# Loading x in contiguous pieces and reordering the front of a state-space mixer kernel

## The chip, the core and the metric

The kernel runs on one core of a Trainium2 chip. The core has five instruction queues that run side by side: TensorE (PE, matrix products), VectorE (DVE), ScalarE (ACT), GpSimd (POOL) and SyncE (SP, which here only issues DMA transfers). Each works through its own instructions in the order in which they are written; they meet through semaphores. The metric is the device time of one execution, in microseconds (us), as the median of several runs. All data is float32.

## The reference

One layer of a diffusion backbone: an S5 state-space mixer over 256 context and 1024 latent tokens in both directions, then a gated output, then a SwiGLU feed-forward part, each behind an RMS norm whose shift, scale and gate come from the conditioning vector. Cut to what matters here:

```python
def rms_norm(x, g):
    return x * rsqrt(mean(x * x, axis=-1) + 1e-6) * g

m_l = split(silu(c)     @ ada_w + ada_b, 6)      # latent tokens
m_c = split(silu(c_ctx) @ ada_w + ada_b, 6)      # context tokens
h_l = rms_norm(x,   norm_mix) * (1 + m_l[1]) + m_l[0]
h_c = rms_norm(ctx, norm_mix) * (1 + m_c[1]) + m_c[0]

def s5_direction(u_ctx, u_lat, ...):             # 64 groups of 16 channels, 64 states each
    lam_bar = exp(lam * exp(log_step))
    b_bar   = (lam_bar - 1) / lam * (b_re + 1j * b_im)
    def run(u, h0):                              # h[t] = lam_bar * h[t-1] + b_bar @ u[t]
        ...                                      # y[t] = Re(c_mat @ h[t])
    y_c, h_c = run(u_ctx, 0)
    y_l, _   = run(u_lat, h_c)                   # the latent scan starts from the context's state

y = (forward + backward) + d * h
g = gelu(y); y = g * sigmoid(g @ w_glu + b_glu)
x = x + m_l[2] * y
h = rms_norm(x, norm_ffn) * (1 + m_l[4]) + m_l[3]
x = x + m_l[5] * ((silu(h @ w1) * (h @ w3)) @ w2)   # 1024 -> 2816 -> 1024
out = rms_norm(x, norm_final)
```

## The kernel before, in words

**Layout.** The token sequence is cut into chunks of 8 sub-steps (T = 8): 128 chunks of x and 32 of the context. A partition row stands for one of 8 sub-steps times 16 channels. The array `U` (in the tile `ru`, 40 KB in each partition) holds for each of the 64 groups 160 columns: 32 of the context, then 128 of x. Eight groups make a *unit* of 5 KB; unit b of `U` is what the later products read.

**Order.** Nothing is scheduled by a planner: the order in which the code is written is the order on each engine, and the tables `PMUL`, `UACT`, `UCTX`, `RSL` and so on say in which turn a step is issued. Tiles that share memory are kept apart by semaphore waits that follow from the order.

**The front** (L150 to L575) does the following.

- SP issues, in this order, lambda (L152), `xT` in four transfers of 1 MB (L156) that land directly in the x columns of `U`, so in pieces of 512 bytes, `ctxT` of 1 MB into `rxa` (L158), the input matrices `bxy`, and `ada_w` in eight transfers of 512 KB (`ada1_load(0)`, L172), and then eight more.
- Row sums of squares, ten tiles (eight of x, two of the context): ACT squares (L204), POOL adds the two halves of each tile, PE multiplies by a block of ones and adds up over the tiles (L206, one product of 512 columns a tile, into `psx` and `psc`). DVE folds the four column groups (L323, L324), one ACT square root for both (L325), DVE reciprocals `rsp` (L535) and `rcp` (L544).
- Modulation rows: `ada1(0, k)`, two PE products for each k (L199), k = 0..7, as the loads arrive.
- Eigenvalues: a long chain of small DVE operations gives lambda-bar; `cmul` then makes by complex products its powers `PW` and the products `CP` = c times lambda-bar^k, in seven calls of four instructions each.
- `lb_dup` (PE L331, ACT L332) spreads `CP` over the partitions as `LB`. `bl_make(hb)` multiplies `LB` (copied by `lb_psum` at L426 or L428) with the input matrices, two 128x1024 products on DVE or, for the half units in `PMUL`, on POOL; `bl_sum` adds them; `bl_tr` (PE L443, ACT L446) transposes the sum into the weights of `sums`.
- `mix_rows`, `mix_turn`, `mix_scale`, `mix_sel`, `mix_cols` (L456, L460, L77, L475/L476, L481) turn the modulation rows into columns of shift and scale.
- `rs_lat(b)` multiplies unit b's x columns by 1/rms (DVE, 128x1024, in place). The context columns are moved from `rxa` into `U` by the same kind of product, units 0 and 1 at one time (L545) and the other six later (L720). `u_act` (ACT L497), `u_lat` (DVE) and `u_ctx` (POOL) then apply scale and shift.

**The sixteen half units.** A loop over hb = 0..15 (a unit has a forward and a backward half) runs, each turn: `sums(hb)` (PE L584 in two parts, evicted by ACT at L590 or L592/L593), `bl_tr(hb + 2)`, `rs_lat` of a later unit where `RSL = {0: 2, 1: 3, 3: 4, 5: 5, 6: 6, 8: 7}` says so, `u_act` and `u_ctx` of a unit by `UACT` and `UCTX`, `pair` (the first step of the scan, on DVE or POOL), `bl_sum(hb + 5)` (a DMA that adds, issued by POOL, L433) and `bl_make(hb + 6)`. At hb = 6 and 8 `pw_full` (PE L386, ACT L388) writes the spread powers `PWF` into the first 4 KB of `rxa`, where `ctxT` was.

**The rest.** After the loop the scan over chunks runs on DVE, then come the output products, the gated part and the feed-forward part, in which PE works.

Of the kernel before, what the change touches and what calls it, by code (L numbers as in the profile page):

```python
# [13 lines left out]
AF = mybir.ActivationFunctionType  # L14
OP = mybir.AluOpType
AX = mybir.AxisListType

P = 128
D = 1024
# [4 lines left out]
T = 8  # L24
G = 64
# [17 lines left out]
def s5_ffn_kernel(tc, a, out):  # L43
# [3 lines left out]
    with ctx:  # L47
# [107 lines left out]
        for h in range(4):  # L155
            SY.dma_start(X[:, 16 * h:16 * h + 16], a["xT"][:, 16 * h:16 * h + 16])  # L156
        ctxT = view(RXa, 0, [G, 32])
# [35 lines left out]
        psx, psc = pw([4, P]), pw([16, 32])  # L193
# [6 lines left out]

        for i in range(10):
            src = X[:, 8 * i:8 * i + 8] if i < 8 else ctxT[:, 32 * i - 256:32 * i - 224]
            jk, po = junk[i % 6], psx if i < 8 else psc
            S.activation(jk.rearrange("p a b -> p (a b)").rearrange("p (g c) -> p g c", c=src.shape[2]), src, AF.Square)  # L204
# [71 lines left out]
        CP = view(RA, 5.5, [T, 2, G])  # L276
# [5 lines left out]
        qi = PW[:, 0, 1]  # L282
# [4 lines left out]
        ts(PW[:, 0, 0], pr, 1.0, ADD)  # L287
# [8 lines left out]
        def cmul(o, x, tmps=(LTa, view(RXc, 0, [256]))):  # L296
# [15 lines left out]

        V.tensor_copy(yb, PW[:, 0])
# [10 lines left out]
        V.tensor_reduce(rsc, psc.rearrange("p g c -> p c g"), AX.X, ADD)  # L324
        S.activation(rsb, rsb, AF.Sqrt, bias=epsc[:, 0:1], scale=1.0 / D)  # L325
# [10 lines left out]
        cmul(PW[:, 7:8], PW[:, 3:4])  # L336
        ada1(0, *range(3, 8))
# [152 lines left out]
        def rs_lat(b):  # L490
            if b < 8:
                gs = slice(8 * b, 8 * b + 8)
                tt(X[:, gs], X[:, gs], bc(rsp, 1, 8), MUL)
# [41 lines left out]
        V.reciprocal(rsp, rsx)  # L535
        rs_lat(0)
        bl_make(1)
# [1222 lines left out]
```

## Time and profile before

| | |
|---|---|
| three runs | 1019.77, 1023.63, 1024.74 us; median 1023.63 us |
| profiled execution | span 1023.7 us from first to last instruction; this is the only time that the page gives for it |
| busy share of the span | PE 94%, PEld 76%, DVE 77%, POOL 75%, ACT 43% |
| mean granted TensorE clock | 0.985 of full speed |
| moved by DMA | 98.95 MB, mean 97 GB/s |

A row of the timeline reads: start, length, engine, line, operation, what is written and what is read, how many instructions are joined in the row, and in brackets the idle time of the engine just before the row and what ended it. "L77" and "L80" are the lines of helpers (two- and three-operand vector operations), so those rows are told apart by their tiles: `ru` is `U`, `rxa` holds `ctxT` and later `PWF`, `c` are the four work regions, `lta`, `ltb`, `lbt` are PSUM tiles with constants. A row of a table of stages gives, for a stretch of time, the busy time of each engine with its number of instructions, then the granted TensorE clock, the mean busy share of the 16 DMA engines and the GB/s that they moved. "PEld" is the loading of weights into TensorE, beside PE.

### The profile page before, as it was taken

What the parts mean: (1) busy time and instruction counts of PE and PEld (TensorE: products, weight loads), DVE (VectorE), ACT (ScalarE), POOL (GpSimd) and SP (SyncE); (2) the same over time, 40 slices, a digit from 0 to 9 for tenths busy, and PEclk for the clock granted to TensorE, in tenths of its full rate; (3) what the DMA queues carried; (4) which work ended last, traced back from release to release, by engine and by line L of the source; (5) the groups of instructions that cost most, each with busy time, mean ns of one, the idle gap of its engine ahead of it and who ended that gap; (6) DMA issues with size and microseconds to landing.
All of it is one profiled execution on the core that took longest, in us unless ns stands there. A gap on an engine that the chain in (4) does not pass through costs nothing. (4 is left out here: it accounts for less than half of the span.)

```text
span 1023.7 us, 18545 instructions
## 1 busy us (share of the span) xinstructions
PE 964.6 (94%) x6988; PEld 774.7 (76%) x6988; DVE 789.9 (77%) x1642; ACT 436.2 (43%) x854; POOL 766.2 (75%) x590
## 2 busy tenths in 40 slices
PE   4987898878999999999999999999999999999996
PEld 1465523768999988877888888888888888888885
DVE  8889699995365778898867768595858778686977
ACT  4476722325353663523334343424334343423337
POOL 4699989992591458879787877778686877778674
PEclk9998999989999999999999999999999999999998
DMA  8865997322623021011212011121212112121205
GB/s 296 313 125 98 280 334 251 99 73 54 238 79 87 2 103 62 21 42 42 82 42 65 32 60 55 49 73 47 78 41 77 38 42 62 42 72 52 72 21 164
DMA packets 48545, 98.95 MB, mean 97 GB/s; under 512 B 4284, under 2 KB 18876, under 8 KB 47176
## 3 DMA queue, kind: packets, MB, share of 16 engines
q1 hardware_dynamic: 43272, 86.64, 25.8%
q0 software_dynamic: 2016, 7.34, 3.8%
q10 hardware_dynamic: 3168, 3.79, 1.1%
q8 instruction: 55, 0.90, 0.4%
q14 instruction: 34, 0.28, 0.1%
HBM read 84.25 MB, written 6.17 MB: 88 GB/s over the span
## 5 line engine op out<-in xcount | busy, mean ns | idle before, releaser
L77 POOL TENSOR_TENSOR c<-rxc,c 128x512 fp32r<-128x512 f32 x128 | 170.4, 1345 | 53.0 <-ACT c L1227 52.8
L1286 PE MATMUL ut<-ra,c 128*128 128x512 f32 x400 | 155.8, 389 | 1.0 <-ACT ra L1227 1.0
L1287 PE MATMUL ut<-ra,c 128*128 128x512 f32 x400 | 155.7, 389 | 0.3 <-DVE ra L77 0.3
L1288 PE MATMUL ut<-ra,c 128*128 128x512 f32 x400 | 155.6, 389 | 0.0
L1227 ACT CAST c<-rxc 128x512 fp32r<-128x512 f32 x128 | 78.9, 622 | 146.3 <-PE xt L1568 51.8
L1568 PE MATMUL xt<-c,c 128*128 128x512 f32 x540 | 129.7, 389 | 0.0
L1568 PEld LDWEIGHTS xt<-c,c 128*128 128x128 f32 x540 | 101.4, 188 | 21.0
L77 DVE TENSOR_TENSOR ru<-ru,xt 128x1024 f32<-128x1024 f32 x90 | 107.0, 1214 | 9.7 <-PE xt L1568 7.2
L77 DVE TENSOR_TENSOR ru<-ut,ru 128x512 f32<-128x512 f32 x98 | 67.1, 686 | 42.6 <-PE ut L1288 37.1
L1286 PEld LDWEIGHTS ut<-ra,c 128*128 128x128 f32 x400 | 75.1, 188 | 17.4 <-ACT ra L1227 1.4
L1287 PEld LDWEIGHTS ut<-ra,c 128*128 128x128 f32 x400 | 75.1, 188 | 16.2 <-issue 0.6
L1288 PEld LDWEIGHTS ut<-ra,c 128*128 128x128 f32 x400 | 75.1, 188 | 15.5
L77 POOL TENSOR_TENSOR c<-rw,c 128x512 fp32r<-128x512 f32 (+1 forms) x29 | 41.7, 1436 | 37.7 <-ACT c L1227 37.0
L1288 PE MATMUL ut<-c,c 128*128 128x512 f32 x160 | 62.4, 390 | 1.3 <-POOL c L77 1.3
L77 POOL TENSOR_TENSOR c<-ru,c 128x512 fp32r<-128x512 f32 (+1 forms) x39 | 55.4, 1420 | 9.3 <-ACT c L1227 4.9
L1286 PE MATMUL ut<-c,c 128*128 128x512 f32 x160 | 62.3, 389 | 0.0
L1287 PE MATMUL ut<-c,c 128*128 128x512 f32 x160 | 62.2, 389 | 0.0
L77 POOL TENSOR_TENSOR rxc<-rxc 128x512 f32<-128x512 f32 x40 | 60.6, 1516 | 1.6
L1568 PE MATMUL ut<-c,c 128*128 128x512 f32 x216 | 51.9, 389 | 0.0
L584 PE MATMUL pv<-ru,c 128*64 128x160 f32 x512 | 44.4, 316 | 7.6 <-POOL ru L77 2.8
L77 DVE TENSOR_TENSOR pe<-pe,ru 128x256 f32<-128x256 f32 x64 | 27.4, 429 | 29.5 <-ACT pe L1127 17.4
L77 DVE TENSOR_TENSOR ru<-ru,ut 128x512 f32<-128x512 f32 x76 | 47.2, 678 | 0.3
(446 smaller groups left out, 2581.8 us busy)
## 6 DMA issues: line engine op xcount, KB each, us to landing
c<-in_ada_w SPq DMA_DIRECT2D x46, 256.0 KB
rxc<-in_w SPq DMA_DIRECT2D x38, 256.0 KB
rxc<-in_w SPq DMA_DIRECT2D x19, 512.0 KB
ru<-in_w SPq DMA_DIRECT2D x11, 512.0 KB
rw<-in_w SPq DMA_DIRECT2D x11, 512.0 KB
ra<-in_ada_w SPq DMA_DIRECT2D x10, 512.0 KB
ra<-in_ada_w SPq DMA_DIRECT2D x18, 256.0 KB
ru<-in_xT SPq DMA_DIRECT2D x4, 1024.0 KB
```

Source lines behind the costliest of these rows:

```text
L77: eng.tensor_tensor(out=o, in0=x, in1=y, op=op)
L584: PE.matmul(pv[64 * (i % 2):64 * (i % 2) + 64, ri, c0:c0 + 160], w[:, i, 64 * ri:64 * ri + 64], U[:, 8 * b + 4 * j + i], start=True, stop= ...
L1227: S.copy(o[0], x)
L1286: PE.matmul(pu, wh, bh, start=start, stop=False)
L1287: PE.matmul(pu, wh, bl, start=False, stop=False)
L1288: PE.matmul(pu, wl, bh, start=False, stop=stop)
L1568: PE.matmul(pd, w[:, cs_], b, start=j in (1, 2, 4) and n == 0, stop=n == 2, skip_group_check=j not in (1, 2, 4))
```

## The change

- `xT` is laid out in DRAM as eight contiguous pieces of 512 KB (one unit each, 4 KB in each partition). Piece i lands in the place of unit i + 1 of `U` (piece 7 in the tile `rw`). `rs_lat(b)` reads piece b there and writes unit b, so it now moves as well as scales; it is still one 128x1024 product.
- The context cannot be moved to unit b + 1 before piece b has been read. A new `ctx_rows(b)` does one unit at a time (128x256): units 0 and 1 early, each later unit right behind `rs_lat` of the unit before it. The two large context products are gone. `ctxT` is stored with the units in reverse order, so unit 7 lies at the start of `rxa`.
- `row_sums`: PE makes four products of 128 columns for each tile where it made one of 512, all into the same 128 (or 4 x 32) columns, so the DVE reduction of `psx` is gone; that of `psc` stays.
- The square root is cut in two, one for x (right behind the squares) and one for the context (behind `lb_dup(0, 0)` and `lb_dup(0, 1)`).
- Powers and products lie in one array `Z`, alternately. Three calls of `cmul` with 2, 3 and 4 stacked products replace six calls; the last one (lambda-bar^8) goes behind `u_lat(0, 4)`; four ACT copies then collect the powers into `PW`.
- `ada1(0, 0..3)` goes between the context's row sums, `ada1(0, 4)` ahead of `lb_dup`, `ada1(0, 5..7)` behind it. `BL1[0]` is added up after `mix_scale(0)`; `lb_dup(1, 0)` and `bl_tr(0)` follow it.

On **VectorE**, from the end of the eigenvalue products to the preparation of half unit 0. Before (`ltb<-r_60 128x128` is the reciprocal for x, `128x32` that for the context, `ru<-rxa,ltb` moves the context, `c_64<-c_64,pv` is the sum for half unit 0):

```order
L323 TENSOR_REDUCE r_60<-pw 128x128
L324 TENSOR_REDUCE r_60<-pw 128x32
L77 TENSOR_TENSOR lta<-ra,ltb 128x128
L77 TENSOR_TENSOR rxc<-ra,ltb 128x128
L77 TENSOR_TENSOR ra<-lta,rxc 128x64 x2
L535 RECIPROCAL ltb<-r_60 128x128
L77 TENSOR_TENSOR ru<-ru,ltb 128x8x128
L77 TENSOR_TENSOR c_64<-c_63,lbt 128x1024
L77 TENSOR_TENSOR pv<-c_63,lbt 128x1024
L77 TENSOR_TENSOR c_64<-c_64,pv 128x1024
L544 RECIPROCAL ltb<-r_60 128x32
L77 TENSOR_TENSOR ru<-rxa,ltb 128x16x32
```

With the change:

```order
L341 RECIPROCAL ltb<-r_60 128x128
L342 TENSOR_REDUCE r_60<-pw 128x32
L77 TENSOR_TENSOR ru<-ru,ltb 128x8x128
L548 RECIPROCAL ltb<-r_60 128x32
L77 TENSOR_TENSOR ru<-rxa,ltb 128x8x32 x2
L77 TENSOR_TENSOR c_64<-c_63,lbt 128x1024
L77 TENSOR_TENSOR pv<-c_63,lbt 128x1024
L77 TENSOR_TENSOR ltb<-prow,r_60 128x2x4 x2
L80 SCALAR_TENSOR_TENSOR ltb<-ltb,r_60 128x2x4
L77 TENSOR_TENSOR ra<-ltb,r_60 128x64 x2
L77 TENSOR_TENSOR c_64<-c_64,pv 128x1024
```

The context's reciprocal and its two products now stand ahead of `bl_make(0)`, and the sum for half unit 0 behind the five small operations of `mix_scale`.

On **ScalarE**, the same place. Before (`r_60<-r_60 128x160` is the square root, L332 evicts `lb_dup`):

```order
L325 ACT_TABLE_LOAD
L325 ACTIVATE r_60<-r_60 128x160
L332 ACTIVATE c_65<-pw 128x8x64
L332 ACTIVATE c_65<-pw,r_60 128x8x64
L426 COPY lbt<-c_65 128x128
```

With the change:

```order
L323 ACT_TABLE_LOAD
L323 ACTIVATE r_60<-pw,r_60 128x128
L337 ACTIVATE c_65<-pw 128x8x64
L337 ACTIVATE c_65<-pw,r_60 128x8x64
L343 ACTIVATE r_60<-r_60 128x32
L433 COPY lbt<-c_65 128x128
```

The context's square root (L343) now stands behind both evictions of `lb_dup`.

On **TensorE**, from the context's row sums on. Before (L206 are row sums, L199 the modulation rows, two for each k, L331 is `lb_dup`):

```order
L199 MATMUL prow<-c_66,r_60 2x512 x2
L206 MATMUL pw<-c_64,r_60 128x512
L199 MATMUL prow<-c_66,r_60 2x512 x2
L199 MATMUL prow<-c_65,r_60 2x512 x2
L331 MATMUL pw<-ra 128x512 x2
L199 MATMUL prow<-c_65,r_60 2x512 x2
```

With the change:

```order
L200 MATMUL prow<-c_66,r_60 2x512 x2
L205 MATMUL pw<-c_64,r_60 128x128 x4
L200 MATMUL prow<-c_66,r_60 2x512 x2
L200 MATMUL prow<-c_65,r_60 2x512 x2
L205 MATMUL pw<-c_64,r_60 128x128 x4
L200 MATMUL prow<-c_65,r_60 2x512 x2
L200 MATMUL prow<-c_63,r_60 2x512 x2
L336 MATMUL pw<-ra 128x512 x2
```

`lb_dup` now stands behind five of the eight modulation rows instead of three, and both context row sums behind the first.

The diff, cut to its core:

```diff
-        for h in range(4):
-            SY.dma_start(X[:, 16 * h:16 * h + 16], a["xT"][:, 16 * h:16 * h + 16])
-        ctxT = view(RXa, 0, [G, 32])
+        xw = [view(RU, 5 * i + 5, [8, P]) for i in range(7)] + [view(RW, 0, [8, P])]
+        for i in range(8):
+            SY.dma_start(xw[i], a["xT"][i])
+        ctxT = view(RXa, 0, [8, 8, 32])
...
-        psx, psc = pw([4, P]), pw([16, 32])
+        psx, psc = pw([P]), pw([4, 32])
...
+        def row_sums(i, po):
+            for n in range(4):
+                PE.matmul(po, blk, junk[i % 6][:, 0, P * n:P * n + P], start=i % 8 == 0 and n == 0, stop=i in (7, 9) and n == 3)
+
         for i in range(10):
...
-            PE.matmul(po.rearrange("p g c -> p (g c)"), blk, jk[:, 0], start=i % 8 == 0, stop=i in (7, 9))
-            if i == 8:
-                ada1(0, 0)
+            if i < 8:
+                row_sums(i, psx)
+            else:
+                ada1(0, 2 * i - 16)
+                row_sums(i, psc.rearrange("p g c -> p (g c)"))
+                ada1(0, 2 * i - 15)
...
+        Z = view(RA, 5.5, [2 * T, 2, G])
+        CP, P1 = Z[:, 0::2], Z[:, 3]
...
-        V.tensor_copy(yb, PW[:, 0])
-        cmul(PW[:, 1:2], PW[:, 0:1])
-        cmul(CP[:, 1:2], CP[:, 0:1])
-        V.tensor_copy(yb, PW[:, 1])
-        cmul(PW[:, 3:4], PW[:, 1:2])
-        cmul(CP[:, 2:4], CP[:, 0:2])
-        V.tensor_copy(yb, PW[:, 3])
-        cmul(CP[:, 4:6], CP[:, 0:2])
-        cmul(CP[:, 6:8], CP[:, 2:4])
-        ada1(0, 1, 2)
-        V.tensor_reduce(rsx, psx.rearrange("p g c -> p c g"), AX.X, ADD)
-        V.tensor_reduce(rsc, psc.rearrange("p g c -> p c g"), AX.X, ADD)
-        S.activation(rsb, rsb, AF.Sqrt, bias=epsc[:, 0:1], scale=1.0 / D)
+        S.activation(rsx, psx, AF.Sqrt, bias=epsc[:, 0:1], scale=1.0 / D)
+        V.tensor_copy(yb, P1)
+        cmul(Z[:, 2:0:-1], Z[:, 0:4:3])
+        V.tensor_copy(yb, Z[:, 1])
+        cmul(Z[:, 4:7], Z[:, 0:3])
+        V.tensor_copy(yb, Z[:, 5])
+        cmul(CP[:, 4:8], CP[:, 0:4])
+        ada1(0, 4)
...
         for i in range(2):
             lb_dup(0, i, pw([512]))
-        cmul(PW[:, 7:8], PW[:, 3:4])
-        ada1(0, *range(3, 8))
+        V.reciprocal(rsp, rsx)
+        V.tensor_reduce(rsc, psc.rearrange("p g c -> p c g"), AX.X, ADD)
+        S.activation(rsc, rsc, AF.Sqrt, bias=epsc[:, 0:1], scale=1.0 / D)
+        ada1(0, *range(5, 8))
...
         def rs_lat(b):
             if b < 8:
-                tt(X[:, gs], X[:, gs], bc(rsp, 1, 8), MUL)
+                tt(X[:, 8 * b:8 * b + 8], xw[b], bc(rsp, 1, 8), MUL)
+                if 0 < b < 7:
+                    ctx_rows(b + 1)
+
+        def ctx_rows(b):
+            tt(Xc[:, 8 * b:8 * b + 8], ctxT[:, 7 - b], bc(rcp, 1, 8), MUL)
...
+        mix_sel(0)
         pt, w_ = bl_tr(0, copy=False)
-        mix_sel(0)
         S.copy(w_[:, 0].rearrange("p i n -> p (i n)"), pt[:, 0])
...
         u_lat(0, 4)
         u_ctx(0)
+        cmul(Z[:, 15:16], Z[:, 5:6])
+        for i, j in ((0, 3), (1, 1), (3, 5), (7, 15)):
+            S.copy(PW[:, i], Z[:, j])
...
-            if hb == 0:
-                tt(Xc[:, 16:], ctxT[:, 16:], bc(rcp, 1, G - 16), MUL)
```

More of the change, by code (lines that the diff above doesn't have):

```diff
@@ L294, in s5_ffn_kernel, with cmul @@
         tt(CP[:, 0, 1], q1, k2, MUL)
-        def cmul(o, x, tmps=(LTa, view(RXc, 0, [256]))):
+        def cmul(o, x, tmps=(LTa, view(RXc, 0, [512]))):
             m = x.shape[1]
@@ L534, in s5_ffn_kernel @@
         tq = None
-        V.reciprocal(rsp, rsx)
         rs_lat(0)
+        V.reciprocal(rcp, rsc)
+        ctx_rows(0)
+        ctx_rows(1)
         bl_make(1)
@@ L542, in s5_ffn_kernel @@
         bl_make(0, o2)
[L543 to L545 removed]
         mix_rows()
         pl1 = pv2()
[L548 removed]
         mix_turn()
         mix_scale(0)
+        tt(BL1[0], BL1[0], o2, ADD)
+        lb_dup(1, 0, pl1[:, 0])
+        mix_sel(0)
         pt, w_ = bl_tr(0, copy=False)
[L552 removed]
         S.copy(w_[:, 0].rearrange("p i n -> p (i n)"), pt[:, 0])
```

20 lines of the change are left out of this document (7 added, 13 removed).

## The prediction

> **What bounds the kernel now.** I read the stages first, then who waits in the stage that the change touches, then the chain of instructions there. The table of stages (columns: stretch, its length, busy time of PE, PEld, DVE, ACT, POOL with their instructions, granted clock, DMA share, GB/s):
>
> ```profile
> 45.00:125.00 80.00, 66.73 (x654) 49.14 (x650) 66.06 (x164) 58.22 (x129) 77.10 (x86) 0.96 0.65 158
> 150.00:190.00 40.00, 35.15 (x742) 16.95 (x742) 40.00 (x229) 10.03 (x24) 38.40 (x31) 1.00 0.62 201
> 640.00:1000.00 360.00, 360.00 (x1590) 298.19 (x1589) 270.47 (x311) 134.67 (x234) 274.24 (x205) 1.00 0.17 54
> ```
>
> From 45 to 125 us, where the sixteen half units are prepared, POOL works 77.1 of 80 us; from 150 DVE works without a gap, in the scan; from 640 to 1000 PE does, 360 of 360 us. So whatever moves POOL at 47 us moves the scan, then PE, then the end, one for one. Inside the first of these stages the timeline shows it closer:
>
> ```profile
> 42.03 4.00 POOL L77 TENSOR_TENSOR c<-c,c 128x1024 f32<-128x1024 f32 x2
> 47.19 4.71 POOL L77 TENSOR_TENSOR c<-c,c 128x1024 f32<-128x1024 f32 x2 [1.15 <-DVE c L77]
> 68.59 1.22 DVE L77 TENSOR_TENSOR c<-c,lbt 128x1024 f32<-128x1024 f32 x1 [3.03 <-DMA c<-c]
> 125.15 1.29 POOL L77 TENSOR_TENSOR rxc<-ra,r 128x256 f32<-128x256 f32 x2 [0.19 <-ACT ra L592]
> ```
>
> POOL's last wait of size is at 47.19: it has finished `bl_make(3)` and waits 1.15 us for DVE to finish `bl_make(2)`. DVE is ahead of POOL afterwards (it idles 3.03 us at 65.6 for a transfer that POOL issues), so DVE work added behind 47 us has cover there. The quantity to forecast is therefore the time at which DVE hands `bl_make(2)` to POOL, 47.1 us now, plus what the new waits do to POOL later.
>
> **The loads.** SP's queue, the squares that wait for it, and the rates at that time:
>
> ```profile
> 1.19 12.11 SPq L156 DMA_DIRECT2D ru<-in_xT  x4
> 25.92 4.43 SPq L172 DMA_DIRECT2D ra<-in_ada_w  x4
> 22.06 2.00 ACT L204 ACTIVATE c<-rxa 128x1024 f32<-128x1024 f32 x2 [0.51 <-DMA rxa<-in_ctxT]
> 3.00:6.00 3.00, 0.00 (x0) 0.00 (x0) 1.72 (x10) 0.65 (x2) 0.00 (x0) 1.00 1.02 345
> 6.00:9.00 3.00, 0.00 (x0) 0.00 (x0) 2.69 (x12) 0.00 (x0) 0.00 (x0) 1.00 0.85 274
> 9.00:12.00 3.00, 0.53 (x1) 0.50 (x2) 2.72 (x16) 2.00 (x2) 1.85 (x2) 1.00 0.81 249
> 12.00:16.00 4.00, 2.96 (x5) 0.71 (x3) 3.79 (x21) 2.00 (x2) 2.04 (x3) 1.00 0.92 291
> 28.00:32.00 4.00, 4.00 (x16) 1.04 (x14) 3.23 (x7) 1.59 (x3) 0.75 (x1) 1.00 1.05 387
> ```
>
> The x pieces of 512 bytes move at 345, 274, 249 and 291 GB/s; the `ada_w` rows, in longer pieces, at 387. Between 3 and 16 us that is 1.04 + 0.82 + 0.75 + 1.16 = 3.77 MB in 13 us; at 387 GB/s it is 9.7 us. So the x pieces in 4 KB gain about 3.3 us, and every later load lands that much sooner: the context at 18.6 instead of 21.95, the eight `ada_w` pieces too: SP's issues from 25.92 on each wait for the transfer eight places before, so k = 1 has landed at 25.9 and the rest follow 1.36 us apart (three such steps and the last issue make the 4.43); k = 0 to 7 land from 24.55 to 34.1 now, from 21.2 to 30.8 then. The page "DMA: Bandwidth & Descriptors" of the Trainium skill, section Specifications, lets a transfer run at line rate from 512 B on; by it these pieces would already be long enough and the gain nothing. The rows (249 and 274 against 387) speak against that, but that stretch is also the start of the program; the third rival has the price, worked out from rows.
>
> **What the front makes of it.** PE and ACT now:
>
> ```profile
> 27.59 1.89 PE L199 MATMUL prow<-c,r 128*2 128x512 f32 x8
> 29.41 1.98 PE L331 MATMUL pw<-ra 128*128 128x512 f32 x4
> 33.90 1.89 PE L199 MATMUL prow<-ra,r 128*2 128x512 f32 x8
> 28.43 0.43 ACT L325 ACTIVATE r<-r 128x160 f32<-128x160 f32 x1 [3.06 <-DVE r L324]
> 31.43 0.69 ACT L332 ACTIVATE c<-pw,r 128x512 f32<-128x512 f32 x1 [0.26 <-PE pw L331]
> ```
>
> Of the modulation rows, one k costs 0.9 us of PE (1.89 for two). The piece for k = 4 lands at about 21.2 + 4 x 1.36 = 26.6. `lb_dup` now stands behind k = 4; it needs 1.98 us and would end at about 26.6 + 0.9 + 2.0 = 29.5, against 31.39, a gain of 1.9 and not 3.3, since it was moved behind two more rows. The last rows end at about 32.2 instead of 35.8. Four products of 128 columns for one of 512 I cost at nothing: they run before 19 us, when PE waits for squares (0.53 of 3 us busy from 9 to 12, 2.96 of 4 from 12 to 16), and the root for x behind them is not wanted before DVE's products end at 25.3; only 6 us more of PE work would come through.
>
> The square root for the context is the catch. It now stands in ACT's queue behind both evictions of `lb_dup`. The second ends 0.74 us behind PE now (31.39 to 32.12), so at about 30.2, and the root takes 0.43: 30.6. DVE stands waiting for it with everything that follows. DVE's rows, and at the end PE's transposes and the ACT copy of half unit 0:
>
> ```profile
> 19.47 0.28 DVE L313 COPY ltb<-ra 128x128 f32<-128x128 f32 x1
> 28.31 0.29 DVE L77 TENSOR_TENSOR lta<-ra,ltb 128x128 f32<-128x128 f32 x1
> 29.09 0.95 DVE L535 RECIPROCAL ltb<-r 128x128 f32<-128x128 f32 x1
> 30.08 1.22 DVE L77 TENSOR_TENSOR ru<-ru,ltb 128x1024 f32<-128x1024 f32 x1
> 32.51 1.22 DVE L77 TENSOR_TENSOR c<-c,lbt 128x1024 f32<-128x1024 f32 x1 [1.21 <-DMA ra<-in_ada_w]
> 36.04 0.35 DVE L544 RECIPROCAL ltb<-r 128x32 f32<-128x32 f32 x1
> 37.37 0.38 DVE L77 TENSOR_TENSOR ltb<-prow,r 128x8 f32<-128x8 f32 x2 [0.26 <-PE prow L460]
> 38.80 0.69 DVE L555 COPY c<-pv 128x512 f32<-128x512 f32 x1 [0.45 <-ACT c L553]
> 44.76 2.35 DVE L77 TENSOR_TENSOR c<-c,lbt 128x1024 f32<-128x1024 f32 x2
> 37.11 1.04 PE L443 MATMUL pv<-r,c 128*128 128x128 f32 x8
> 38.19 0.58 ACT L553 COPY c<-pv 128x512 f32<-128x512 f32 x1 [0.71 <-PE pv L443]
> ```
>
> Stacked products need about as many elements but fewer starts. Six calls and two folds took DVE from 19.47 to 28.3; three calls of 2, 3 and 4 products I estimate at 5.9 us with their copies (0.29 for a 128x128 product, less for each one stacked on it), so they end at 25.3. The x reciprocal (0.95), the fold for the context and `rs_lat(0)` (1.22) end at 28.1, 3.2 us sooner than now (31.3). Then DVE idles until the root at 30.6: 2.5 us of this lead are lost. From there I add up: reciprocal and two `ctx_rows` (each a quarter of a 128x1024 product, some 0.4) to 31.75; `bl_make(0)`, two products, 34.15; `mix_scale`, five operations as small as that at 37.37, 1.0, 35.15; the sum for half unit 0, one more 128x1024 product, 36.4; PE's transposes to 37.5 and the ACT copy to 38.2 (1.04 and 0.58, as in the last two rows), so that the DVE copy that stood at 38.80 starts at 38.2. That is a gain of 0.6 us there, and `u_ctx(0)` on POOL gains 1.0, which POOL does not need: it waits for DVE afterwards.
>
> Behind this copy, DVE had 8.31 us of work to the end of `bl_make(2)` (38.80 to 47.11). The change puts into the same stretch the `cmul` for lambda-bar^8 (four instructions; the same ones took 0.9 us around 28.31, beside the wait) and `ctx_rows(2)`, 0.4: 9.6 us. So `bl_make(2)` ends at 38.2 + 9.6 = 47.85 instead of 47.11, and POOL goes on **0.7 us later** than now; its wait grows from 1.15 to about 2.9 us, as its own work before it ends a microsecond sooner. Bounds: if stacking saves nothing and the root comes a microsecond later, +1.7; if the root is there as soon as `rs_lat(0)` ends, -1.8 (2.5 gained). ACT's four copies of powers (some 0.3 each) stand ahead of the eviction that `sums(0)` waits for; that start moves by 0.4 at the most, and POOL does not wait for it.
>
> **The new wait at half unit 6.** `PWF` lies where the context of units 7 to 4 lies now. Before, the context had been read in the loop's first turn; now unit 7 is read only behind `rs_lat(6)`. The rows there:
>
> ```profile
> 81.06 0.57 ACT L388 COPY rxa<-pv 128x512 f32<-128x512 f32 x1
> 82.26 1.21 DVE L77 TENSOR_TENSOR ru<-ru,ltb 128x1024 f32<-128x1024 f32 x1
> 81.67 1.31 PE L584 MATMUL pv<-ru,c 128*64 128x160 f32 x16 [0.90 <-ACT rxa L388]
> 85.19 1.60 POOL L77 TENSOR_TENSOR ru<-ru,r 128x256 f32<-128x256 f32 x2
> 86.84 4.54 PE L584 MATMUL pv<-ru,c 128*64 128x160 f32 x32 [2.83 <-POOL ru L77]
> 84.00:86.00 2.00, 0.01 (x1) 0.00 (x0) 1.90 (x7) 1.90 (x5) 1.96 (x4) 1.00 0.00 0
> 88.00:90.00 2.00, 2.00 (x18) 1.80 (x16) 2.00 (x4) 0.67 (x1) 1.92 (x4) 0.50 0.32 59
> 93.23 1.01 ACT L446 COPY c<-pv 128x1024 f32<-128x1024 f32 x1 [1.08 <-PE pv L443]
> ```
>
> The ACT copy at 81.06 has to wait for `rs_lat(6)` (82.26 + 1.21) and `ctx_rows` of units 6 and 7 (0.4 each, the first behind `rs_lat(5)`): 84.3, so ACT stands 3.25 us. Behind it stand the evictions of `sums(7)`, PE's second part of `sums(7)` (already today it waits 0.90 us for this copy), the transposes for half unit 9 and `u_act`. PE stands from 80.8 to 84.9. What takes it up: PE had a hole of 2.83 us at 84.0 to 86.84, in which it waited for POOL's `u_ctx(4)`, and the clock fell to 0.50 behind that hole. The hole now comes before the work instead of behind it. With a full clock behind it, `sums(8)` needs about 2 x 1.31 instead of 4.54 us, and half of that gain stays, since its second part then waits for the `u_act` that the stall has moved: the ACT copy at 93.23 comes 1.0 us earlier. With half the clock for as long as now it comes 1.0 later, the 1.31 us of `sums(7)` being slowed as well. I take +0.3, as the longer hole is nearer to the second. The page "TensorE: Matmul & The Clock Gate" of the Trainium skill, Part 1, has the clock halve after an idle window of about 3.4 us that runs freely; the 0.50 behind 2.83 us agrees roughly, and by it a hole of 4.1 us would halve it too.
>
> **The sum.** 0.7 at POOL's restart and 0.3 at half unit 6 make +1.0 us on the profiled 1023.7, which stands within 0.1 of the median of the runs (1023.63); on the median that is **1024.6 us**, no difference that a measurement of this kernel can tell (I count within 0.5%, 5.1 us, as the same).
>
> **The rivals.** *The loads' gain arrives whole* (faster). DVE does not wait for the root, or the added work lies under waits that I have not seen: POOL goes on 3.3 us sooner, and half unit 6 brings 1.0: 1023.7 - 4.3 = 1019.4. For it: nearly everything up to 39 us hangs on loads. Against: POOL waits for DVE, and DVE has more to do than before between 38 and 47.
>
> *The wait for the context's last unit goes through* (slower). If POOL needs an eviction or a row of `U` that stands behind the stalled ACT copy, the 3.25 us are POOL's, and at half the clock the 1.31 us of `sums(7)` take as much again. With the 0.7 of the front: 1023.7 + 0.7 + 3.25 = 1027.7, up to 1029.0. It decides as soon as `sums(8)` starts later than 88 us. For it: POOL has no slack from 47 to 125. Against: what POOL does next, `u_ctx(4)` at 85.19, waited for nothing and needs nothing of the stalled copy.
>
> *Contiguous pieces do not move faster* (slower). Then x lands as now, and the reordered front, which I let start 3.3 us earlier, starts as now with the added rows ahead of `lb_dup` and the root behind it: +0.7 + 3.3 + 0.3 = 1028.0. For it: 345 GB/s in the first window with the same short pieces, so the lower rates after it may have another reason. Against: with the longer rows the DMA engines moved 387 for four microseconds on end.
>
> **How the numbers follow.** Forecast 0.45 (1022.5 to 1026.5 by its bounds), loads whole 0.25, wait goes through 0.18, pieces no faster 0.12. The runs of before spread over 5 us themselves, so of the first rival about two in five fall below -0.5%, with a little of the forecast 0.13; of the two slow ones about a third lie beyond +0.5%, with a little of the forecast 0.12; the rest, 0.75, is the same. The range of 1018.5 to 1029.0 takes in all four.
>
> **What would show it.** In the profile after: SP's x issues end by 10 us instead of 13.3 and the context's squares start at about 18.7 (if at 22, the third rival). The context's reciprocal on DVE shows an idle time of some 2.5 us, released by ACT's square root at about 30.6 (if none, the first). POOL's wait for DVE at 47 us is nearer 3 than 1 us, and the row behind it starts at 47.9. The ACT copy of `PWF` waits about 3 us for DVE at 81 to 84, and `sums(8)` starts before 88 us. POOL's row at 125.15 comes at about 126.1. I am wrong if POOL's row starts before 46 or after 49.5, or if POOL shows new waits between 85 and 125.

## The result and the profile after

The changed kernel takes 1025.97 us (median of 20 runs, 1024.01 to 1028.77) against 1023.70 us (20 runs of before beside it, 1019.77 to 1027.57): a ratio of 1.0021, 95% interval 1.0011 to 1.0031, so 1.1 to 3.2 us slower. Within the bound of 0.5% that the forecast counts as the same, this is no change, as forecast, though the interval lies clear of 1; the forecast was +1.0 us. (One run below, of the last kernel of experiment 8, took 1210.98 us at a mean clock of 0.751, in a slow state, and is left out of that kernel's median and ratio.) The profiled execution took 1025.3 us, with a span of 1023.5; time less span was 1.8 us in most runs. The profile of before had 1023.7 as its span, nearly the same. By that difference of 1.8 us its time would be about 1025.5 (an estimate), well above the median of 1023.7: the prediction, which set the span of 1023.7 beside a median of 1023.63, compared a span with a time. That is the first thing to be explained: two profiles with equal spans, of kernels whose medians differ by 2.3 us.

The rates of the loads in the changed kernel (table of stages, the columns of the one shown for before):

```profile
3.00:6.00 3.00, 0.00 (x0) 0.00 (x0) 1.61 (x9) 1.27 (x3) 0.00 (x0) 1.00 1.05 395
6.00:9.00 3.00, 1.17 (x5) 1.17 (x6) 2.67 (x12) 2.48 (x3) 2.40 (x2) 1.00 1.03 419
9.00:12.00 3.00, 3.00 (x16) 3.00 (x15) 2.74 (x15) 2.34 (x4) 2.96 (x4) 1.00 1.03 411
12.00:16.00 4.00, 3.79 (x33) 3.60 (x32) 3.79 (x20) 3.02 (x3) 3.90 (x4) 1.00 1.03 422
```

The loads now move at 395 to 422 GB/s, faster than the 387 of the later loads that the forecast had taken for x. (The last stretch also holds the start of the context, as the last squares of x start at 14.49 us.) The timeline of the same kernel, in the front and at half unit 6, to the first row of the scan (the last one, an ACT copy that starts with it):

```profile
21.57 10.51 SPq L173 DMA_DIRECT2D ra<-in_ada_w  x8
27.09 1.98 PE L336 MATMUL pw<-ra 128*128 128x512 f32 x4
30.04 0.36 DVE L548 RECIPROCAL ltb<-r 128x32 f32<-128x32 f32 x1 [2.02 <-ACT r L343]
37.27 0.69 DVE L567 COPY c<-pv 128x512 f32<-128x512 f32 x1 [1.80 <-ACT c L565]
46.77 4.72 POOL L77 TENSOR_TENSOR c<-c,c 128x1024 f32<-128x1024 f32 x2 [2.74 <-DVE c L77]
69.31 1.26 PE L450 MATMUL pv<-r,c 128*128 128x128 f32 x8 [2.89 <-DMA c<-c]
85.66 0.58 ACT L395 COPY rxa<-pv 128x512 f32<-128x512 f32 x1 [1.24 <-DVE ru L77]
89.78 1.65 PE L599 MATMUL pv<-ru,c 128*64 128x160 f32 x16
92.33 0.88 POOL L440 DMA_DIRECT2D c<-c  x1 [1.08 <-ACT ru L509]
94.90 1.01 ACT L453 COPY c<-pv 128x1024 f32<-128x1024 f32 x1 [0.34 <-PE pv L450]
126.83 1.29 POOL L77 TENSOR_TENSOR rxc<-ra,r 128x256 f32<-128x256 f32 x2 [1.14 <-ACT ra L607]
132.18 0.36 ACT L784 COPY kt<-r 128x240 f32<-128x240 f32 x1 [4.75 <-DVE ra L77]
```

The waits named ahead are there: VectorE waits 2.02 us for the context's square root, POOL 2.74 us for VectorE at 46.77, ScalarE 1.24 us for the context of unit 7. TensorE has a wait that was not named: 2.89 us at 69.31, for a transfer that adds up an input matrix, where the kernel before waited 1.50. Two more rows were named as signs against the forecast: `sums(8)` starts at 89.78, later than the 88 us that were to decide for the second rival, and POOL has a new wait between 85 and 125 us, 1.08 us at 92.33 for a `u_act` of ScalarE. The row that starts the scan stood at 130.51 in the profile of before:

```profile
130.51 0.36 ACT L771 COPY kt<-r 128x240 f32<-128x240 f32 x1 [4.76 <-DVE ra L77]
```

So the scan starts 1.67 us later, although POOL's restart came 0.42 us *earlier* (46.77 against 47.19). Most of this shift arises at half unit 6: the ACT copy at 93.23 in the profile of before stands at 94.90 now, 1.67 later, and from there to the end of the loop everything keeps its distance. POOL, by contrast, waits 1.14 us for ScalarE at 126.83, where it had waited 0.19.

### The profile page after: what moved, and what is told of

The parts are those of the page before. It is cut to its first block, busy times and chain, and to the rows that moved or that the text cites. A ratio compares the mean times of both kernels' runs of the same rounds, so it can differ in the third digit from the quotient of the medians.

```text
span 1023.5 us, 18669 instructions
## 1 busy us (share of the span) xinstructions
PE 966.2 (94%) x7048; PEld 782.6 (76%) x7048; DVE 789.0 (77%) x1635; ACT 437.7 (43%) x859; POOL 766.7 (75%) x590
## 4 chain that ended last, share of the span: by engine, by line
PE 69%; DVE 19%; POOL 4%; ACT 3%; issue 3%; DMA 2%; SPq 0%; ACTq 0%; DVEq 0%; POOLq 0%
PE xt L1581 12%; PE ut L1301 12%; PE ut L1299 12%; PE ut L1300 11%; DVE ra L77 5%; PE ut L1581 5%; DVE ru L77 3%; PE pe L1112 3%; PE pe L1110 3%; PE pe L1111 3%; DVE ltb L77 3%; POOL c L77 2%; DVE ltc L77 2%; PE pe L935 1%; PE pv L599 1%
## 5 line engine op out<-in xcount | busy, mean ns | idle before, releaser
L77 DVE TENSOR_TENSOR pe<-pe,ru 128x256 f32<-128x256 f32 x64 | 27.4, 428 | 29.5 <-ACT pe L1140 17.4
L599 PEld LDWEIGHTS pv<-ru,c 128*64 128x64 f32 x512 | 36.0, 144 | 15.9 <-ACT ru L509 5.2
```

The costliest lines, as they stand in the source:

```text
L77: eng.tensor_tensor(out=o, in0=x, in1=y, op=op)
L599: PE.matmul(pv[64 * (i % 2):64 * (i % 2) + 64, ri, c0:c0 + 160], w[:, i, 64 * ri:64 * ri + 64], U[:, 8 * b + 4 * j + i], start=True, stop= ...
```

## The experiments

Twelve more measurements were made, in three groups, each group on one chip beside its own runs of the kernel before: 11 or 12 runs for each, 5 for the kernel of experiment 2. Two marks are read in every profile: **R**, the start of POOL's row behind its wait for VectorE (47.19 in the profile of before), and **S**, the ACT copy that starts with the scan (130.51). S - R says what the sixteen half units cost, span - S what lies behind.

| kernel | R | S | S - R | span - S | time against before (95% interval) |
|---|---|---|---|---|---|
| before, profile of the forecast | 47.19 | 130.51 | 83.32 | 893.2 | |
| before, again | 44.97 | 128.14 | 83.17 | 893.5 | 1.0004 (0.9995 to 1.0013) |
| before, PWF copy later | 44.87 | 127.62 | 82.75 | 893.8 | 0.9998 (0.9986 to 1.0010) |
| before, context by units | 45.16 | 130.15 | 84.99 | 894.1 | 1.0019 (1.0007 to 1.0030) |
| changed | 46.77 | 132.18 | 85.41 | 891.3 | 1.0021 (1.0011 to 1.0031) |
| changed, again | 46.80 | 131.85 | 85.05 | 891.2 | 1.0020 (1.0005 to 1.0035) |
| changed, PWF copy later | 46.93 | 129.99 | 83.06 | 891.8 | 1.0019 (1.0005 to 1.0033) |
| the same, again | 46.62 | 131.94 | 85.32 | 893.6 | 1.0030 (1.0019 to 1.0040) |
| changed, PE kept busy | 46.97 | 131.40 | 84.43 | 891.9 | 1.0055 (1.0040 to 1.0071) |
| changed, x in 512 bytes | 49.62 | 133.37 | 83.75 | 891.9 | 1.0049 (1.0036 to 1.0061) |
| changed, scaling earlier | 48.39 | 131.70 | 83.31 | 893.6 | 1.0010 (0.9998 to 1.0021) |
| the same, gap filled | 47.91 | 131.06 | 83.15 | 892.4 | 0.9990 (0.9978 to 1.0002) |
| changed, front reordered | 44.15 | 129.19 | 85.04 | 891.1 | 0.9994 (0.9985 to 1.0002) |
| front reordered and scaling earlier | 43.75 | 126.92 | 83.17 | 891.8 | 0.9981 (0.9972 to 0.9991) |

**1. The two kernels once more.** No edit; a second profile of each.

> The changed kernel itself, once more, for a second profile. Two theories of where its extra time arises. Stall theory: the copy of PWF at half unit 6 waits for the context of unit 7 (1.24 us idle in the first profile), and with that the evictions and transposes behind it. Clock theory: TensorE's hole from 66.4 to 69.3 us, in which it waits for a transfer that adds up an input matrix, is longer than before (2.9 us against 1.5) and TensorE then works at half the clock from 70 to 77 us, so that the ScalarE copy of the transposes at 78.17 comes 3.3 us late. Stall: scan starts at about 132 us again whatever the clock was at 70 to 77. Clock: at about 132 only if the clock is 0.50 there again; if it is full, at 130.5 or before. Time against before 1.002 by both.

> The kernel before itself, once more: two other executions with its loads and nearly its front moved x at 345 to 380 GB/s and restarted POOL at 44.9 and 45.2 us, where the profile of the forecast had 249 to 345 GB/s and 47.19. If that profile was the unusual one: x at about 350 GB/s, POOL's restart at 44.8 to 45.3 and the scan at 127.5 to 128.5 here; if not, 47 and 130.5. Time 1.000 within 0.001: what two sets of runs of one kernel differ by.

The changed kernel repeated itself: R 46.80, S 131.85. Its clock was 0.67 at 70 to 72, 0.50 at 72 to 74 and full again at 76, so its half clock was shorter than in the first profile and S was 0.3 us earlier; this alone does not tell the two theories apart. The kernel before did *not* repeat itself:

```profile
23.28 1.72 SPq L172 DMA_DIRECT2D ra<-in_ada_w  x2
44.97 4.71 POOL L77 TENSOR_TENSOR c<-c,c 128x1024 f32<-128x1024 f32 x2 [0.62 <-DVE c L77]
88.78 1.01 ACT L446 COPY c<-pv 128x1024 f32<-128x1024 f32 x1 [0.36 <-PE pv L443]
122.78 1.29 POOL L77 TENSOR_TENSOR rxc<-ra,r 128x256 f32<-128x256 f32 x2
128.14 0.36 ACT L771 COPY kt<-r 128x240 f32<-128x240 f32 x1 [4.76 <-DVE ra L77]
```

(The rows at 88.78 and 122.78 are the ones that stood at 93.23 and 125.15 in the first profile; they are needed further down.) Its table of stages shows why R came sooner:

```profile
3.00:6.00 3.00, 0.00 (x0) 0.00 (x0) 1.55 (x9) 0.64 (x2) 0.00 (x0) 1.00 1.05 372
6.00:9.00 3.00, 0.00 (x0) 0.00 (x0) 2.69 (x12) 1.76 (x2) 0.62 (x1) 1.00 1.02 348
9.00:12.00 3.00, 2.31 (x3) 1.12 (x4) 2.72 (x16) 1.98 (x3) 2.47 (x3) 1.00 1.01 347
12.00:16.00 4.00, 4.00 (x7) 1.43 (x6) 3.76 (x22) 2.27 (x3) 3.50 (x4) 1.00 1.01 356
```

The pieces of 512 bytes move at 347 to 372 GB/s, not at 249 to 345. Two more executions with the same loads (the kernels "before, PWF copy later" and "before, context by units") had 345 to 380. The one execution on which the forecast rested was the unusual one of four, with loads that landed 2.6 us late: SP's second run of `ada_w` issues starts at 23.28 here, at 25.92 there. Against the usual execution, POOL's restart in the changed kernel is 1.8 us *later* (46.8 against 45.0), and S is 3.7 to 4.0 us later.

**2. x in 512 bytes again.** The changed kernel with one part undone:

```diff
-        xw = [view(RU, 5 * i + 5, [8, P]) for i in range(7)] + [view(RW, 0, [8, P])]
+        xw = [X[:, 8 * i + 8:8 * i + 16] for i in range(7)] + [view(RW, 0, [8, P])]
```

> The changed kernel with one part undone: seven of the eight x pieces land in the x columns of the unit behind, so in pieces of 512 bytes again; order, waits and front stay. If the 4 KB pieces are what moves faster: x at 350 GB/s instead of 420, the modulation rows and POOL's restart 1.5 to 2 us later (48.3 to 48.8), time 1.0005 to 1.002 above the changed kernel. If 512 bytes are as fast: x at 420, restart at 46.8, time as the changed kernel.

Its rates and POOL's restart, from two views:

```profile
3.00:6.00 3.00, 0.00 (x0) 0.00 (x0) 1.79 (x11) 0.65 (x2) 0.00 (x0) 1.00 0.97 271
6.00:9.00 3.00, 0.13 (x1) 0.13 (x1) 2.69 (x12) 2.11 (x2) 1.27 (x1) 1.00 1.07 316
9.00:12.00 3.00, 3.00 (x15) 3.00 (x16) 2.72 (x17) 1.90 (x2) 2.53 (x2) 1.00 1.12 333
12.00:16.00 4.00, 3.25 (x26) 2.87 (x25) 3.76 (x24) 2.46 (x4) 3.26 (x4) 1.00 1.13 364
```

```profile
49.62 4.71 POOL L77 TENSOR_TENSOR c<-c,c 128x1024 f32<-128x1024 f32 x2 [2.60 <-DVE c L77]
```

The short pieces are slower, and they cost what the loads lose: R 2.8 us later than in the changed kernel, and 1.0049 of before where the changed kernel had 1.0020. That is 2.9 us, more than the 0.5 to 2 expected. This execution's 271 and 316 GB/s are again below the 347 of the usual ones; all five runs lie between 1027.88 and 1029.53 us, so it was no odd one out. Why the short pieces are slower here than in the usual execution of before is not shown. So the long pieces work, and this part of the change is a gain. The third rival is out. The page "DMA: Bandwidth & Descriptors" of the Trainium skill, section Specifications, has pieces of 512 bytes at line rate; the trace has 347 GB/s from 9 to 12 us for the kernel before against 411 for the changed one, and the measurement decides.

**3. The wait for the context alone.** The kernel before, with the context moved by units behind the row scaling:

```diff
                 tt(X[:, gs], X[:, gs], bc(rsp, 1, 8), MUL)
+                if 0 < b < 7:
+                    ctx_rows(b + 1)
...
-        tt(Xc[:, 0:16], ctxT[:, 0:16], bc(rcp, 1, 16), MUL)
+        ctx_rows(0)
+        ctx_rows(1)
...
-            if hb == 0:
-                tt(Xc[:, 16:], ctxT[:, 16:], bc(rcp, 1, G - 16), MUL)
```

(`ctxT` is stored in reverse, as in the change.)

> The kernel before with one part of the change: the context is moved unit by unit behind the row scaling of the unit before it, and stored in reverse order, so that the PWF copy has to wait for unit 7 as in the changed kernel; loads, front and clock at 70 to 77 us as before. Stall theory: the copy waits about 3 us at 81 to 84, the scan starts 1 to 3 us later than before (131.5 to 133.5), time 1.001 to 1.003. Clock theory, and the forecast's term of 0.3 us: the wait is taken up, scan within 0.5 us of 130.5, time 1.000 to 1.0005.

```profile
45.16 4.70 POOL L77 TENSOR_TENSOR c<-c,c 128x1024 f32<-128x1024 f32 x2 [0.84 <-DVE c L77]
82.88 0.58 ACT L388 COPY rxa<-pv 128x512 f32<-128x512 f32 x1 [3.09 <-DVE ru L77]
130.15 0.36 ACT L776 COPY kt<-r 128x240 f32<-128x240 f32 x1 [4.76 <-DVE ra L77]
```

The front is that of before (R 45.16), the stall of ScalarE has the size that the forecast gave it (3.09, forecast 3.25), and S - R grows from 83.17 to 84.99: 1.8 us. The time is 1.0019 of before. The wait is not taken up. The clock theory is out for this kernel: the clock was 1.00 from 70 to 80 here. It was 0.50 from 84 to 88, behind the stall; a drop at that place alone is not the cost, for the kernel before of experiment 5 had 0.57 in the same stretch, without the stall, and an S - R of 82.75.

**4. TensorE kept busy in its hole.** The changed kernel with 16 products more, ahead of the transposes for half unit 6:

```diff
             pt, w_ = pv2(), Win[hb % 3]
+            for i in range(16 if hb == 6 else 0):
+                PE.matmul(pt[:, i // 4 % 2, P * (i % 4):P * (i % 4) + P], blk, ident, start=True, stop=True)
```

> The changed kernel with 16 more products of 128x128 (about 2.2 us, results overwritten) in TensorE's hole at 66 to 69 us, so that it is not idle there; the wait of the PWF copy stays. Clock theory: clock 1.00 at 70 to 77, the ScalarE copy of the transposes that came at 78.17 comes at about 75, the scan starts at 130.8 or before, time 0.9996 to 1.0005 of before. Stall theory: the copy of PWF waits as long or longer (2 to 3 us, since ScalarE arrives sooner), the scan starts at about 132, time 1.002.

```profile
67.06 3.84 PE L449 MATMUL pv<-r 128*128 128x128 f32 x32 [0.45 <-ACT ra L607]
70.73 1.04 PE L452 MATMUL pv<-r,c 128*128 128x128 f32 x8
85.23 0.58 ACT L395 COPY rxa<-pv 128x512 f32<-128x512 f32 x1 [2.50 <-DVE ru L77]
```

The clock stayed at 1.00 from 66 to 86, and the PWF copy then waited 2.50 instead of 1.24 us, as the stall theory said; S was 0.5 to 0.8 us earlier. But the products took 3.84 us instead of the 2.2 that I had counted, so the real transposes began later than in either profile of the changed kernel, and the time rose to 1.0055. The profiled execution took 1025.04 us, the median of this kernel is 1030.10 (ten of its twelve runs lie at 1028.7 or above); where the other 5 us go its profile does not show. Inconclusive as to the time, clear as to the wait.

**5. The PWF copy one half unit later**, in the changed kernel (twice) and in the kernel before:

```diff
-            if hb in (6, 8):
-                pw_full(hb // 2 - 3)
+            if hb in (7, 8):
+                pw_full(hb - 7)
```

> The changed kernel with the first copy of PWF one half unit later (7 instead of 6), when the context of unit 7 has long been read. Stall theory: no wait of that copy, the scan starts at about 130.1 us (POOL's restart was 0.4 us earlier than before), time 0.9996 of before. Clock theory: half the clock at 70 to 77 us stays, the scan starts at 131.5 or later, time 1.0015 to 1.002.

> The changed kernel with the copy of PWF one half unit later, once more: its profiled execution had no stall, a scan that starts 83.06 us behind POOL's restart and a span of 1021.8 us, yet its runs are 1.0019 of before. If single executions differ in the transfers and in TensorE's clock ahead of the scan, this profile shows the scan 1 to 2 us later than the first (131 to 132) and half the clock at 70 to 77; if the loss is behind the scan, it starts at 130 again and the span is 1023 to 1026. Time 1.001 to 1.002.

> The kernel before with the copy of PWF one half unit later and nothing else: a control for that move. If the move costs nothing in itself, time 0.999 to 1.0005 of before, scan within 0.5 us of 83.3 behind POOL's restart. If it costs time of its own (two PWF copies in half units that follow each other), 1.001 to 1.002, and then it says nothing on the stall in the changed kernel.

In the kernel before the move costs nothing (0.9998). In the changed kernel it takes the wait away (the copy at 85.61 waits for nothing) and S - R falls to 83.06 in the first profile, as the stall theory said, and yet the time does not fall. The second profile, from a set of runs at 1.0030, shows how S can be late without the stall:

```profile
46.62 4.72 POOL L77 TENSOR_TENSOR c<-c,c 128x1024 f32<-128x1024 f32 x2 [2.76 <-DVE c L77]
112.49 1.94 PE L450 MATMUL pv<-r,c 128*128 128x128 f32 x8 [3.00 <-DMA c<-c]
131.94 0.36 ACT L784 COPY kt<-r 128x240 f32<-128x240 f32 x1 [4.76 <-DVE ra L77]
```

TensorE, now ahead, waits 3.00 us at 112 for one of the transfers that POOL issues to add up the input matrices, and the table of stages has its clock at 0.50 from 112 to 116 and 0.69 to 120. The stall was taken away and another wait, with a clock drop behind it, came in its place in this execution. That this is what holds the median up is argued from one profile, not shown.

**6. The scaling of units 5 and 6 earlier.** The wait goes away in another manner, by reading the context sooner, in VectorE's idle time at half unit 3:

```diff
-        RSL = {0: 2, 1: 3, 3: 4, 5: 5, 6: 6, 8: 7}
+        RSL = {0: (2,), 1: (3,), 3: (4, 5, 6), 8: (7,)}
```

> The changed kernel with the row scaling of units 5 and 6, and with them the context of units 6 and 7, at half unit 3, in VectorE's idle time at 65 to 69 us; nothing waits for the context at half unit 6 any more, and the copy of PWF stays where it was. Stall theory: scan starts 83.1 to 83.5 us behind POOL's restart at 46.8 (before 83.3, changed kernel 85.0 to 85.4), time 0.999 to 1.000 of before. Rival (the rest of the change costs the time, through the front or TensorE's clock): scan no longer late, but time 1.0015 to 1.002 all the same, with the loss behind the scan's start.

```profile
20.37 1.68 PE L200 MATMUL prow<-c,r 128*2 128x512 f32 x4 [2.35 <-DMA c<-in_ada_w]
48.39 4.71 POOL L77 TENSOR_TENSOR c<-c,c 128x1024 f32<-128x1024 f32 x2 [2.74 <-DVE c L77]
85.54 0.57 ACT L395 COPY rxa<-pv 128x512 f32<-128x512 f32 x1
131.70 0.36 ACT L784 COPY kt<-r 128x240 f32<-128x240 f32 x1 [4.75 <-DVE ra L77]
```

S - R is 83.31: the stall's 1.8 us are gone, although the clock was at half from 72 to 76:

```profile
72.00:76.00 4.00, 3.77 (x24) 3.29 (x26) 2.65 (x10) 2.19 (x7) 3.92 (x9) 0.50 0.69 131
```

The clock theory, by which S is late for that, is out here too; in the second kernel of experiment 8 the clock was 0.50 to 0.53 from 70 to 74, with an S - R of 83.17. The time is 1.0010 of before, between what the two theories named, and 1.0 us less than the changed kernel (1.0020 to 1.0021); the intervals overlap. R is late in this execution for a reason that the first row shows: with x summed early, TensorE waits 2.35 us for the first modulation weights, and its clock was 0.58 from 20 to 24 behind that hole, so that the modulation rows and `lb_dup` took longer.

**7. The same, with VectorE's gap filled.** VectorE's copy, which waited 1.80 us at 37.27, goes behind `u_lat` and the last product of powers; ScalarE copies the columns of shift and scale first:

```diff
-        S.copy(w_[:, 0].rearrange("p i n -> p (i n)"), pt[:, 0])
         mix_cols(0, S)
-        V.tensor_copy(w_[:, 1].rearrange("p i n -> p (i n)"), pt[:, 1])
+        S.copy(w_[:, 0].rearrange("p i n -> p (i n)"), pt[:, 0])
...
         cmul(Z[:, 15:16], Z[:, 5:6])
+        V.tensor_copy(w_[:, 1].rearrange("p i n -> p (i n)"), pt[:, 1])
```

> As rs456, and VectorE's idle 1.80 us in the front is filled: its copy of the second half of the weights goes behind u_lat and the last product of powers, and ScalarE copies the columns of shift and scale ahead of the weights. If VectorE's path to bl_make(2) sets POOL's restart, POOL restarts 1.5 to 1.9 us sooner than in rs456 (at about 45.0). If POOL's restart carries through to the end, time 1.5 to 1.9 us below rs456 (0.9975 to 0.9985 of before); if TensorE and ScalarE set the end of the loop, less than 0.8 us below it.

The time falls by 2.2 us against experiment 6 on the same chip (1023.35 against 1025.56), somewhat more than the 1.8 us of idle time; the intervals of the two overlap a little. R in its profile, 47.91, shows only 0.5 of it, since the clock fell there too (0.50 from 20 to 24, 0.68 to 28), for longer than in experiment 6.

**8. The front in another order**, without and with experiment 6. Beside the edit of experiment 7:

```diff
             else:
-                ada1(0, 2 * i - 16)
                 row_sums(i, psc.rearrange("p g c -> p (g c)"))
-                ada1(0, 2 * i - 15)
+        ada1(0, 0, 1, 2, 3)
...
         cmul(Z[:, 4:7], Z[:, 0:3])
+        V.tensor_reduce(rsc, psc.rearrange("p g c -> p c g"), AX.X, ADD)
+        S.activation(rsc, rsc, AF.Sqrt, bias=epsc[:, 0:1], scale=1.0 / D)
         V.tensor_copy(yb, Z[:, 5])
         cmul(CP[:, 4:8], CP[:, 0:4])
-        ada1(0, 4)
...
         V.reciprocal(rsp, rsx)
-        V.tensor_reduce(rsc, psc.rearrange("p g c -> p c g"), AX.X, ADD)
-        S.activation(rsc, rsc, AF.Sqrt, bias=epsc[:, 0:1], scale=1.0 / D)
-        ada1(0, *range(5, 8))
+        ada1(0, *range(4, 8))
...
-        mix_scale(0)
         tt(BL1[0], BL1[0], o2, ADD)
+        mix_scale(0)
```

> The changed kernel with its front put in another order, the wait at half unit 6 left as it is: both context row sums ahead of the modulation rows, the context's square root before the last product of powers, lb_dup behind four modulation rows, the sum for half unit 0 ahead of mix_scale, the copy of the second half of its weights behind u_lat. Front theory (the two idle times of VectorE, 2.0 and 1.8 us, put POOL's restart at 46.8 instead of 45): no idle time on VectorE from 26 to 36, POOL's restart at 43 to 44. The PWF wait stays at 1 us or more. Time 0.999 to 1.0005 of before if POOL's restart carries through; 1.001 to 1.002 if the PWF wait alone sets the loss.

> front_only and rs456 together: no idle time of VectorE in the front, no wait for the context at half unit 6. POOL's restart at 43 to 44, the scan 83 us behind it at 126 to 127, against 45 and 128 in the usual execution of the kernel before. Time 0.997 to 0.999 of before if both theories hold; 0.999 or more if what the scan gains is lost behind it (TensorE's clock, the loads of the scan).

The last kernel's rows:

```profile
28.16 0.36 DVE L546 RECIPROCAL ltb<-r 128x32 f32<-128x32 f32 x1
34.25 1.41 DVE L77 TENSOR_TENSOR ru<-ru,ltb 128x512 f32<-128x512 f32 x2 [0.53 <-PE ltb L480]
43.75 4.71 POOL L77 TENSOR_TENSOR c<-c,c 128x1024 f32<-128x1024 f32 x2 [2.33 <-DVE c L77]
126.92 0.36 ACT L782 COPY kt<-r 128x240 f32<-128x240 f32 x1 [4.76 <-DVE ra L77]
```

The context's reciprocal no longer waits for the square root, the 2.02 and 1.80 us of idle time are down to one of 0.53, and POOL restarts at 43.75, 3.0 us ahead of the changed kernel and 1.2 ahead of the usual execution of the kernel before. With the wait at half unit 6 left in (2.15 us of ScalarE; R 44.15, S 129.19) the time is 0.9994 of before; with it gone, **0.9981 (0.9972 to 0.9991)**: 1022.04 against 1023.44 us by the medians, the fastest version, ahead of the kernel before by more than its measurement is uncertain. The two kernels of this pair differ by 1.3 parts in a thousand, 1.3 us, which fits the wait at half unit 6, though their intervals overlap; S moves by 2.3 us, of which 1.87 are S - R.

## Why the prediction was right, and where its terms were not

**What bounds the kernel.** Right for the front: POOL waits for VectorE at its restart in all fourteen profiles, and VectorE's chain sets it. Behind it, POOL is the bound in the kernel before, but with hardly any margin, and no longer in the changed one. Two chains end at S. On POOL, the row at 122.78 in experiment 1's profile of before starts 77.81 us behind R, with no wait of POOL from 55 us on, and S follows 5.36 us later. On TensorE and ScalarE, the ACT copy at 88.78 lies 39.36 us ahead of S there, so this chain had about 2 us to spare; in the profile of the forecast the same copy (93.23) lies 37.28 us ahead and POOL waits 0.19 us, so it had none. In the three kernels with the plain stall (the changed one, the one before with the context by units, the one with the front reordered) that copy lies 37.27 to 37.29 us ahead of S and POOL waits 1.14 to 1.52 us for ScalarE at the end: there TensorE and ScalarE set S. The sum followed POOL alone; POOL's 77.1 of 80 us busy says nothing of how close the other chain is.

**The loads.** Right in direction, wrong in size: "the x pieces in 4 KB gain about 3.3 us" was worked out from an execution whose loads were slow. In the usual execution SP's second run of `ada_w` issues starts at 23.28; in the changed kernel at 21.57. The gain is 1.7 us. The other error had the opposite sign: the pieces move at 395 to 422 GB/s, not at 387, so that against the execution of the forecast (25.92) the gain is 4.4.

**The front.** The order of events came out as forecast: `lb_dup` ends at 29.07 (forecast 29.5), the context's root is the catch and VectorE idles 2.02 us for it (2.5), POOL waits 2.74 us (2.9) and restarts at 46.77 (47.85). As the loads came a microsecond sooner than forecast, everything did. The idle time of VectorE ahead of the copy, which the sum had in it but did not name as a wait, is 1.80 us at 37.27: it stands for ScalarE's copy, because the sum for half unit 0 stands behind `mix_scale`. The term "0.7 us later" was +0.7 against a restart that was itself 2.2 us late; against the usual 44.97 it is +1.8. This term was 1.1 us too small.

**The wait at half unit 6.** The place and the size of the stall were right (3.25 us forecast; 3.09 in experiment 3, 1.24 and 2.07 in the changed kernel, where ScalarE arrives later). "I take +0.3" is the step that failed most, by 1.6 us: S - R grew by 1.7 to 2.2 us in each of the three kernels that have the plain stall (with the shorter stall of experiment 2, 0.78 us, by 0.4 to 0.6). The overlap that the sum counted on, TensorE's hole of 2.83 us moved ahead of the work (0.88 only in experiment 1's profile of before), did not repay the stall, since TensorE and ScalarE had at most 2 us to spare. The second rival's mechanism was the true one, at about half its price: the delay went through ScalarE and TensorE and reached POOL as waits for ScalarE, at 92.33 and at the end of the loop. That is one of the two things by which the prediction said it would be wrong.

**The sum.** +1.8 in the front and +1.9 in the loop would be 3.7 us, and S is indeed that much later than in the usual execution of before. The median says +2.3. What gives 2 us back lies behind the scan: span - S is 893.2 to 894.1 in four profiles with the old front and 891.1 to 891.9 in seven of the ten with the new one. Where this arises is read from three marks in the same profiles, here of the kernel before (first profile) and then of the changed one: two transfers that SP issues, and the first cast of the gate weights on VectorE.

```profile
221.83 0.35 SPq L893 DMA_DIRECT2D rxa<-mbd  x1
248.68 4.57 SPq L830 DMA_DIRECT2D ra<-kd  x4
260.61 0.69 DVE L1075 CAST c<-rxa 128x1024 fp32r<-128x1024 f32 x1 [3.85 <-DMA rxa<-in_w_glu]
```

```profile
223.47 0.35 SPq L906 DMA_DIRECT2D rxa<-mbd  x1
247.59 4.17 SPq L843 DMA_DIRECT2D ra<-kd  x4
258.46 0.69 DVE L1088 CAST c<-rxa 128x1024 fp32r<-128x1024 f32 x1 [1.46 <-DMA rxa<-in_w_glu]
```

The first lies 91.3 us behind S in both, the second 118.2 and 115.4. So the gain is there before the gate weights are asked for, and VectorE's shorter wait for them (1.46 against 3.85 us) is not where it starts. Between these two marks TensorE's clock fell to 0.60 to 0.68, in a stretch of 4 us between 228 and 236, in all four profiles with the old front, and in neither profile of the changed kernel. The three of the new front at 892.4 to 893.6 had a drop there too (0.50 to 0.65), and so had that of experiment 2 (0.70). The second mark follows the drop in all fourteen profiles: 116.0 to 118.5 us behind S in the eight with it, 114.9 to 115.7 in the six without. That the drop costs the time, and why the new front mostly avoids it, no run shows; it stays open.

So the forecast, +1.0 us and no measurable change, came within 1.3 us of the measured +2.3, and the bound of 0.5% was never in question. That it came so close is in part luck: its two terms were 1.1 and 1.6 us too small, and a third, of -2 us behind the scan, was not in it. Its case came true in the front; in the loop the second rival's mechanism did.

## What to carry to other kernels

Before a gain is worked out from a rate in a profile, look whether that rate is the usual one: one more profiled execution of the kernel before would have shown 347 GB/s where the forecast read 249, and the changed kernel's front as a loss of 1.8 us where one pair of profiles shows a gain of 0.4. When data are made to land in a place that is still in use, ask which later writer now waits for the last reader: here a copy four half units away did. And when a load gets faster, walk down the queue of each engine behind it: the square root, put behind two evictions that it has nothing to do with, kept 2 us of the gain, and a different order of the same instructions, with the wait at half unit 6 removed as well, turned +0.2% into -0.2%. Last, before a delay on one engine is taken as hidden, measure how far that engine's chain is ahead of the one that bounds: here it was 0 to 2 us ahead, beside a stall of 3.

## What the runs showed of the hardware

- Pieces of 512 bytes into on-chip memory moved at 345 to 380 GB/s in three executions and at 249 to 345 and 271 to 364 in two others; pieces of 4 KB at 371 to 422 in all nine that have them (up to 16 us, the start of the context included). The long pieces were faster and also steadier.
- TensorE's granted clock fell to between 0.5 and 0.6 behind holes of 1.9 to 4.1 us, not each time: the wait for the first modulation weights at 18 to 20 us lowered it in experiments 6 and 7 (2.35 and 2.40 us), and not in the changed kernel (2.22) or in the first profile of experiment 5's changed kernel (2.52). The page "TensorE: Matmul & The Clock Gate" of the Trainium skill, Part 1, has the drop after at least one idle window of about 3.4 us that runs freely; here shorter holes were enough. The runs of one kernel differ by up to 8 us (before: 1019.77 to 1027.57), more than the whole change is worth; how much of that is the clock, no run shows.
- Sixteen float32 products of 128x128 put in to keep TensorE busy took 3.84 us, 0.24 each. The trace has them as 32 records, two for each product; a record took 0.12 us, about as long as one of the eight transposes behind them (1.04 us for eight records).
